# Output projection in seven half-sized products, gain and bias of the first norm on transposed rows, x added by accumulating loads

## The chip, the cores and the metric

One of the cores of a Trainium2 chip runs the whole kernel. The metric is device time in microseconds (us) of one launch. The engines are TensorE (PE, matrix products, with PEld for its weight loads), VectorE (DVE), ScalarE (ACT), GpSimd (POOL, which also issues the DMAs of the software queue) and SyncE (SP, which issues the others). Each executes its own list of instructions in order; semaphores tie the lists together. Matrix products write PSUM banks of 128x512, everything else lives in SBUF tiles of 128 partitions, and weights stream in from DRAM.

## What is computed

One layer of a decoder trunk: 512 tokens, width 1024. Three attention branches are gated and merged (not shown), then:

```python
def layer_norm(x, g, b):
    mu = xf.mean(-1, keepdims=True)
    var = jnp.square(xf - mu).mean(-1, keepdims=True)
    return ((xf - mu) * lax.rsqrt(var + LN_EPS) * g + b).astype(x.dtype)
...
m = mixer(x, ...)          # ends with merged @ w_out
x = layer_norm(DEEPNORM_ALPHA * x + m, ln1_g[i], ln1_b[i])
hid = jax.nn.relu(x @ w_up[i])
c = jnp.square(hid) @ w_down[i]
ple = jax.nn.sigmoid(x @ w_ple_gate[i]) * (p[i] @ w_ple[i])
x = layer_norm(DEEPNORM_ALPHA * x + c + ple, ln2_g[i], ln2_b[i])
```

Everything is float32. The change touches `merged @ w_out`, the first norm, and `p @ w_ple`.

## The kernel before, in words

**Products.** A float32 product is made of three products in a reduced format: each operand is split into a high part h (a cast, ACT: `wh` for weights, line 243) and a remainder l (a subtraction, DVE: `wl`, line 245), and h·h + h·l + l·h is summed in PSUM. Large products are done by Strassen's scheme in seven half-sized products, p = 1 to 7 in the order 1, 2, 7, 6, 4, 5, 3 (`seven`), each for two row tiles r; a half-sized product of one row tile is 12 PE products of 128x512. The summed weight blocks that p5, p6, p7 and p3 need are made in DRAM by the software queue (`sum_steps`), paced by a credit that each item of the program adds to, or by adding a second block onto a loaded one in SBUF (`chained`, line 180).

**The output projection** (`wout_items`, line 897) does not use that scheme: for both column halves and four row tiles tt it runs 24 PE products (lines 909 to 911) from `merged_T`, the split and transposed merge (`turn_item`). The eviction (line 917, DVE) computes y = ALPHA·x + product with its row sum; x comes in eight loads `xn` of 128x512 (256 KB each) by POOL. After the second half of a row tile `ln1_gen(tt)` starts.

**The first norm** (`layer_norm_act`, line 861): row mean (DVE, L866), sum of squares of each half (ACT, L868, into `junk`), variance (DVE, L870 and L871), the power -1/2 (POOL, L872), then for each half (x - mean)·g (DVE, L874) and ·r + b (DVE, L882). After a count of steps by tt, PE transposes the row tile (eight 128x128, line 946); ACT and DVE split it into `x1hT`, `x1lT` (L952, L953), and ACT copies it to `x1r` (L959), of which the operands of the gate's later products are summed (`x_forms`: L1163 and following; t7, t6 and t4 are those of p7, p6 and p4).

**Around it.** The eight items `ple` (p @ w_ple, lines 977 to 979, evicted by ACT at L983) stand behind the output projection and fill PE while the last rows are normed. Then the gate x @ w_ple_gate runs as seven half-sized products in the order 2, 1, 7, 6, 4, 5, 3 (lines 1040 to 1042): its p2 and p1 need the transposed rows alone, p7 needs t7. `gate_rest` multiplies gate and `ple` and adds ALPHA·x1 later.

**Order.** Program order of each engine follows from the recording: an item's eviction is recorded after the next item's products have begun, casts of coming weights are pumped between items, and generators in `pending` take one step at a time. A wait thus holds back all that was recorded behind it on the same engine. POOL issues its DMAs in that order as well, and each of them also waits for the landing of the one eight places ahead of it.

## Time and profile before

| what | value |
|---|---|
| median of 3 runs | 1036.45 us (1035.87 to 1036.88) |
| the profiled execution | 1036.02 us |
| its span, first to last instruction | 1033.9 us |
| mean granted TensorE clock | 0.998 |
| instructions on PE, DVE, ACT, POOL | 5434, 1412, 1012, 271 |
| first product of the output projection | 606.63 us into the span |
| first product of the gate's p7 | 681.46 us into the span |

A time that follows "start" in the timeline counts from the span's first instruction. A group line gives source line, engine, operation, out<-in with shapes, count, then busy time in us and mean duration in ns. The duration of a PE product is longer than the distance to the next one, since products overlap; what a product costs is that distance. The same holds for short operations on ACT and DVE.

### The profile page before, as it was taken

The numbers are of one execution on the slowest core, as the hardware profiler recorded it, in microseconds if no ns is written. First come the engines' busy times: TensorE is split into PE (matmuls) and PEld (weight loads), VectorE is DVE, ScalarE is ACT, GpSimd is POOL, SyncE is SP. The second block draws the span as 40 slices with busy tenths as digits, with TensorE's granted clock in tenths as the row PEclk, the third lists the DMA queues.
The fourth block names the chain that finished last, engine by engine and source line by source line (L and its number), as shares of the span: only waits on it lengthen the run. The fifth ranks groups of instructions, "written<-read, shape, count | busy, mean of one in ns | idle before, by whom it ended". The sixth has DMA issues, their size and how long they took to land.

```text
span 1033.9 us, 15019 instructions
## 1 busy us (share of the span) xinstructions
PE 1025.6 (99%) x5434; PEld 880.3 (85%) x5434; DVE 786.4 (76%) x1412; ACT 592.9 (57%) x1012; POOL 180.5 (17%) x271
## 2 busy tenths in 40 slices
PE   9999999999999999999999999999999999999997
PEld 6888888889888888888888888889999899899886
DVE  7888667769764657779688895798768777777966
ACT  7565544536434646576575743776666556566651
POOL 0002411121211232411011040111111111111001
PEclk9999999999999999999999999999999999999999
DMA  8349969485976999977789895479999999998612
GB/s 310 122 158 272 286 185 220 113 289 151 279 191 214 268 283 292 254 193 199 229 270 222 269 324 197 141 214 336 336 293 312 296 324 339 306 310 273 227 61 81
DMA packets 71321, 249.19 MB, mean 241 GB/s; under 512 B 8808, under 2 KB 9592, under 8 KB 71248
## 3 DMA queue, kind: packets, MB, share of 16 engines
q0 software_dynamic: 32464, 116.21, 45.0%
q1 hardware_dynamic: 38208, 131.13, 35.1%
q8 instruction: 42, 0.69, 0.3%
q10 hardware_dynamic: 576, 0.92, 0.2%
q14 instruction: 31, 0.25, 0.1%
HBM read 246.10 MB, written 98.59 MB: 333 GB/s over the span
## 4 chain that ended last, share of the span: by engine, by line
PE 97%; DVE 2%; ACT 0%; issue 0%; DVEq 0%
PE mm L87 10%; PE mm L89 10%; PE mm L88 10%; PE at L1300 4%; PE at L1301 4%; PE at L1302 4%; PE at L618 3%; PE at L620 3%; PE at L619 3%; PE mm L495 2%; PE mm L497 2%; PE mm L496 2%; PE at L89 1%; PE at L88 1%; PE at L87 1%; PE at L911 1%
## 5 line engine op out<-in xcount | busy, mean ns | idle before, releaser
L243 ACT CAST wh<-raw 128x1024 fp32r<-128x1024 f32 x257 | 268.4, 1049 | 236.3 <-PE mm L88 126.1
L245 DVE TENSOR_TENSOR wl<-raw,wh 128x1024 fp32r<-128x1024 f32 x257 | 312.2, 1222 | 118.3 <-ACT wh L243 117.5
L87 PE MATMUL mm<-xhT,wh 128*128 128x512 f32 x302 | 119.1, 394 | 0.0
L89 PE MATMUL mm<-xhT,wl 128*128 128x512 f32 x302 | 118.3, 392 | 0.0
L88 PE MATMUL mm<-xlT,wh 128*128 128x512 f32 x302 | 118.2, 391 | 0.0
L1300 PE MATMUL at<-wh,hh 128*128 128x512 f32 x188 | 73.7, 392 | 0.0
L1301 PE MATMUL at<-wl,hh 128*128 128x512 f32 x188 | 73.7, 392 | 0.0
L1302 PE MATMUL at<-wh,hl 128*128 128x512 f32 x188 | 73.1, 389 | 0.0
L87 PE MATMUL mm<-x1hT,wh 128*128 128x256 f32 x256 | 72.8, 284 | 0.0
L88 PE MATMUL mm<-x1lT,wh 128*128 128x256 f32 x256 | 72.4, 283 | 0.0
L89 PE MATMUL mm<-x1hT,wl 128*128 128x256 f32 x256 | 72.4, 283 | 0.0
L89 PEld LDWEIGHTS mm<-xhT,wl 128*128 128x128 f32 x302 | 56.7, 188 | 12.0
L87 PEld LDWEIGHTS mm<-xhT,wh 128*128 128x128 f32 x302 | 56.7, 188 | 11.3 <-PE mm L497 0.2
L88 PEld LDWEIGHTS mm<-xlT,wh 128*128 128x128 f32 x302 | 56.8, 188 | 10.8
L87 PEld LDWEIGHTS mm<-x1hT,wh 128*128 128x128 f32 x256 | 48.9, 191 | 1.9
L88 PEld LDWEIGHTS mm<-x1lT,wh 128*128 128x128 f32 x256 | 48.9, 191 | 1.5
L89 PEld LDWEIGHTS mm<-x1hT,wl 128*128 128x128 f32 x256 | 48.9, 191 | 0.0
L1118 POOL DMA_DIRECT2D usum<-in_wu_dram x32 | 28.4, 933 | 106.8 <-DMA usum<-usum 44.4
L1118 POOL DMA_DIRECT2D dsum<-in_wd_dram x28 | 25.4, 928 | 103.0 <-DVE wl L245 63.2
L1302 PEld LDWEIGHTS at<-wh,hl 128*128 128x128 f32 x188 | 35.3, 188 | 7.7
L1300 PEld LDWEIGHTS at<-wh,hh 128*128 128x128 f32 x188 | 35.5, 189 | 6.1
L1301 PEld LDWEIGHTS at<-wl,hh 128*128 128x128 f32 x188 | 35.5, 189 | 5.7
(628 smaller groups left out, 2673.9 us busy)
## 6 DMA issues: line engine op xcount, KB each, us to landing
usum<-in_wu_dram POOLq DMA_DIRECT2D x48, 512.0 KB, 9.1
dsum<-in_wd_dram POOLq DMA_DIRECT2D x42, 512.0 KB, 9.0
raw<-in_wt_dram SPq DMA_DIRECT2D x38, 512.0 KB, 5.4
raw<-usum SPq DMA_DIRECT2D x32, 512.0 KB, 7.8
raw<-dsum SPq DMA_DIRECT2D x28, 512.0 KB, 6.6
raw<-in_wd_dram SPq DMA_DIRECT2D x25, 512.0 KB, 5.8
raw<-in_wu_dram SPq DMA_DIRECT2D x24, 512.0 KB, 7.0
raw<-in_wv_dram SPq DMA_DIRECT2D x18, 512.0 KB, 5.7
```

The source lines that it names most:

```text
L87: nc.tensor.matmul(ps, wh, xh, start=start, stop=False, skip_group_check=True)
L88: nc.tensor.matmul(ps, wh, xl, start=False, stop=False, skip_group_check=True)
L89: nc.tensor.matmul(ps, wl, xh, start=False, stop=stop, skip_group_check=True)
L243: i = nc.scalar.copy(h, raw)
L245: i = nc.vector.tensor_sub(lo, raw, h.bitcast(F32))
L618: nc.tensor.matmul(ps, h[:, q], c["h"][:, n], start=go, stop=False, skip_group_check=True)
L619: nc.tensor.matmul(ps, h[:, q], c["l"][:, n], start=False, stop=False, skip_group_check=True)
L620: nc.tensor.matmul(ps, lo[:, q], c["h"][:, n], start=False, stop=end, skip_group_check=True)
L1118: i = nc.gpsimd.dma_start(o, i, accum_op=OP.add, max_dma_last_dim=4096)
L1300: nc.tensor.matmul(ps, h[:, q], c["h"][:, s], start=go, stop=False, skip_group_check=True)
L1301: nc.tensor.matmul(ps, h[:, q], c["l"][:, s], start=False, stop=False, skip_group_check=True)
L1302: nc.tensor.matmul(ps, lo[:, q], c["h"][:, s], start=False, stop=end, skip_group_check=True)
```

## The change

1. The output projection goes through `seven`. Three of its seven products end in PSUM banks of their own, and a tile of the result is put together in SBUF from two or three evictions. `turn_item` writes plain copies `mr` of the transposed merge; `wout_forms` sums and splits them into the operands m7, m6, m4, m5, m3 (ten casts, ten remainders, six sums).
2. The sums of weight blocks for it are `wsum` in DRAM (eight steps more of 512 KB), and p7 and p3 add a block onto a loaded one.
3. x is carried as x + y/ALPHA, so the norm uses EPS/ALPHA². The tiles of p1 and p7 are evicted by ACT into `wx`, scaled by 1/ALPHA, and x is added to each by an accumulating load of 256 KB; the other four half rows are loaded as `xn` before.
4. The norm normalises without gain and bias by two ACT operations of 128x512 (scale r, bias -mean·r, which POOL multiplies). Gain and bias are put on the transposed rows by eight ACT operations of 128x128 a row tile, with columns from `lncol`; `x1hT` is cast from their result. The row-major x1 gets gain and bias in `gate_rest`, by a multiplication and an addition on DVE for each half row tile.
5. Two of the eight `ple` items move between p2 and p7 of the projection. The loads of ln1_g and ln1_b come later, the steps of the weight sums are paced faster, and the counts of steps before the transposes become 3, 3, 5, 6.

```diff
+        def wout_forms():
+            r11, r12, r21, r22 = [[merged_T[h, th, kp] for kp in range(2)] for h in range(2) for th in range(2)]
...
+            r7 = [slot("mr") for _ in range(2)]
+            for kp in range(2):
+                nc.vector.tensor_sub(r7[kp], r22[kp], r12[kp])
+            form(7, r7)
...
-                hi, lo = slot("mh", F32R), slot("ml", F32R)
-                nc.scalar.copy(hi, ps)
-                nc.vector.tensor_sub(lo, ps, hi.bitcast(F32))
-                merged_T[h, th, kp] = (hi, lo)
+                if not th:
+                    hi, lo = slot("mh", F32R), slot("ml", F32R)
+                    nc.scalar.copy(hi, ps)
+                    nc.vector.tensor_sub(lo, ps, hi.bitcast(F32))
+                    wo_forms.setdefault(1 + h, []).extend(by_k(hi, lo))
+                t = slot("mr")
+                nc.scalar.copy(t, ps)
+                merged_T[h, th, kp] = t
...
-            it.setdefault("rate", 2.8 if j < 25 else 0.0 if j < 31 else 2.6)
+            it.setdefault("rate", 2.8 if j < 25 else 0.0 if j < 31 else 2.6 if j < 49 else 3.2)
...
-            for tt in range(4):
+            for tt in (0, 1) if h else (2, 3):
                 t = slot("xn")
...
+            def operand(cs, p, kp):
+                return chained(cs, p, kp, [a["wo"][kp, i].rearrange("p k n -> p (k n)") for i in range(4)], wsum[kp])
+
+            def row(tt, half, t, ps, sign):
...
+                i = nc.vector.scalar_tensor_tensor(t, ps, sign * INV, t, op0=OP.mult, op1=OP.add,
+                                                   accum_out=x1sum[tt][:, half:half + 1])
...
+            def later(ps, r):
+                for _ in range(3):
+                    yield
+                row(r, 0, s.pop((1, r)), ps, 1.0)
+
+            def done(ps, p, r):
+                if p in (1, 7):
+                    t = s[p, r] = slot("wx")
+                    nc.scalar.activation(t, ps, AF.Copy, scale=INV if p == 1 else -INV)
+                    src = a["xn"][:, r, 0:512] if p == 1 else a["xn"][:, 2 + r, 512:1024]
+                    nc.gpsimd.dma_start(t, src, accum_op=OP.add, max_dma_last_dim=4096)
+                elif p == 2:
+                    pending.append(later(ps, r))
+                elif p == 6:
+                    t = s[6, r] = xn.pop((r, 1))
+                    nc.vector.scalar_tensor_tensor(t, ps, -INV, t, op0=OP.mult, op1=OP.add)
+                elif p == 4:
+                    row(r, 1, s.pop((6, r)), ps, -1.0)
+                elif p == 5:
+                    row(2 + r, 1, s.pop((7, r)), ps, -1.0)
+                else:
+                    row(2 + r, 0, xn.pop((2 + r, 0)), ps, 1.0)
...
+                if (p, r) == (2, 1):
+                    ple_items(range(FIRST))
...
-            layer_norm_act([x1[tt, 0], x1[tt, 1]], x1sum[tt], "ln1_g", "ln1_b", fin)()
-            for _ in range((2, 3, 6, 8)[tt]):
+            nc.vector.tensor_scalar(nmu, sm[:, 0:1], sm[:, 1:2], -1.0 / D, op0=OP.add, op1=OP.mult)
+            for h in range(2):
+                nc.scalar.activation(junk, ts[h], AF.Square, bias=nmu, accum_out=sq[:, h:h + 1])
+            nc.vector.tensor_scalar(r, sq[:, 0:1], sq[:, 1:2], 1.0 / D, op0=OP.add, op1=OP.mult)
+            nc.vector.tensor_scalar(r, r, EPS / ALPHA ** 2, None, op0=OP.add)
+            nc.gpsimd.tensor_tensor(r, r, mhalf, OP.pow)
+            nc.gpsimd.tensor_tensor(c, nmu, r, OP.mult)
+            for h in range(2):
+                nc.scalar.activation(ts[h], ts[h], AF.Identity, scale=r, bias=c)
+            for _ in range((3, 3, 5, 6)[tt]):
                 yield
...
+                    for k in range(2):
+                        n = 4 * h + 2 * kp + k
+                        nc.scalar.activation(r3[:, k, :], tp[:, (2 * kp + k) * P:(2 * kp + k) * P + P], AF.Identity,
+                                             scale=lncol[:, n:n + 1], bias=lncol[:, 8 + n:9 + n])
+                    if tt < 2 or h:
+                        ks = slice(4 * h + 2 * kp, 4 * h + 2 * kp + 2)
+                        o = x1T["b"][:, ks, q]
+                        nc.scalar.copy(o, r3)
+                        nc.vector.tensor_sub(x1Tl["b"][:, ks, q], r3, o.bitcast(F32))
...
                     t = x1[tt, half]
+                    nc.vector.tensor_mul(t, t, lnc["ln1_g"][half])
+                    nc.vector.tensor_add(t, t, lnc["ln1_b"][half])
...
+            todo.extend(two_steps(wsum[m], a["wo"][m]) for m in range(2))
...
-            if 12 <= n < wout_at + 8:
+            if 12 <= n < STEPS_TO:
...
-            if n == wout_at - 1:
+            if n == ple_at:
                 ln_consts("ln1_g", "ln1_b")
```

The order lists show what comes of it. Names are out<-in with a number for each tile; the brackets name the semaphores waited for. First ACT, between row tile 1's and row tile 2's norm. Before, from the copies of row 0 to the squares (L868) of row 2:

```order
L952 CAST x1hT<-at_6329 128x4x128 [waits PE_49]
L952 CAST x1hT<-at_6336 128x4x128 [waits PE_49]
L959 COPY x1r_6343<-at_6329 128x2x128 [waits DVE_49]
L959 COPY x1r_6345<-at_6329 128x2x128
L243 CAST wh_6441<-raw_5975 128x1024 [waits DMAHW2_49,PE_49]
L959 COPY x1r_6347<-at_6336 128x2x128 [waits DVE_49]
L959 COPY x1r_6349<-at_6336 128x2x128
L868 ACTIVATE junk_6352,lsq_6351<-xn_5927,lnm_6353 128x512
L243 CAST wh_6447<-raw_6033 128x1024 [waits DMAHW3_49,PE_49]
L868 ACTIVATE junk_6352,lsq_6351<-xn_5984,lnm_6353 128x512 [waits Activation_49]
```

Now, from row 1's transposed tiles (at_6475, at_6488) to the squares (L999) and the normalising (L1005) of row 2:

```order
L1032 CAST x1hT<-x1r_6437 128x2x128 [waits Activation_49]
L1027 ACTIVATE x1r_6442<-at_6475,lncol 128x128
L1027 ACTIVATE x1r_6452<-at_6488,lncol 128x128 [waits PE_49]
L1032 CAST x1hT<-x1r_6442 128x2x128 [waits Activation_49]
L1027 ACTIVATE x1r_6452<-at_6488,lncol 128x128
L1027 ACTIVATE x1r_6457<-at_6488,lncol 128x128
L1032 CAST x1hT<-x1r_6452 128x2x128 [waits Activation_49]
L1027 ACTIVATE x1r_6457<-at_6488,lncol 128x128
L999 ACTIVATE junk_6505,lsq_6501<-xn_5937,lnm_6502 128x512 [waits DVE_49]
L1032 CAST x1hT<-x1r_6457 128x2x128 [waits Activation_49]
L999 ACTIVATE junk_6505,lsq_6501<-wx_6239,lnm_6502 128x512 [waits Activation_49]
L243 CAST wh_6568<-raw_6362 128x1024 [waits DMAHW7_49,PE_49]
```

Row 2's squares stand behind all of row 1's work on the transposed tiles, and that work is eight small operations and four casts in place of two casts and four copies.

On POOL, around the powers of the four row tiles (`lr` with `mhalf`). Before, the gain and bias loads and then the powers:

```order
L857 DMA ln_b_6020<-in_ln_b_dram 128x512 [waits DMASW1_49]
L1648 DMA pTr_6065<-in_pT_dram 128x512 [waits DMASW2_49,PE_49]
L1648 DMA pTr_6067<-in_pT_dram 128x512 [waits DMASW3_49,PE_49]
L872 TENSOR_TENSOR lr_6253<-lr_6253,mhalf 128x1 [waits DVE_49]
L872 TENSOR_TENSOR lr_6293<-lr_6293,mhalf 128x1 [waits DVE_49]
L1118 DMA dsum_1_145<-in_wd_dram 128x1024 [waits DMASW4_49,DVE_49]
L872 TENSOR_TENSOR lr_6357<-lr_6357,mhalf 128x1 [waits DVE_49]
```

Now (6330, 6377, 6503 and 6538 are row tiles 0 to 3):

```order
L1002 TENSOR_TENSOR lr_6377<-lr_6377,mhalf 128x1 [waits DVE_49]
L1003 TENSOR_TENSOR lc_6378<-lnm_6376,lr_6377 128x1 [waits Pool_49]
L895 DMA ln_g_6528<-in_ln_g_dram 128x512 [waits DMASW1_49,PE_49]
L895 DMA ln_g_6529<-in_ln_g_dram 128x512 [waits DMASW2_49,PE_49]
L895 DMA ln_b_6532<-in_ln_b_dram 128x512 [waits DMASW3_49,PE_49]
L1002 TENSOR_TENSOR lr_6503<-lr_6503,mhalf 128x1 [waits DVE_49]
L895 DMA ln_b_6533<-in_ln_b_dram 128x512
L1003 TENSOR_TENSOR lc_6504<-lnm_6502,lr_6503 128x1 [waits Pool_49]
L1002 TENSOR_TENSOR lr_6538<-lr_6538,mhalf 128x1 [waits DVE_49]
L1003 TENSOR_TENSOR lc_6539<-lnm_6537,lr_6538 128x1 [waits Pool_49]
```

The loads of gain and bias went behind row 1's power, and the last of them, ln_b_6533, behind row 2's; each power is followed by a product.

On DVE, in the queue ahead of the gate's t7. Before, from row 3's normalising (L882) to t7's sums (L1163) and remainder:

```order
L882 SCALAR_TENSOR_TENSOR xn_5929<-xn_5929,lr_6397,ln_b_6019 128x512 [waits Pool_49]
L882 SCALAR_TENSOR_TENSOR xn_5986<-xn_5986,lr_6397,ln_b_6020 128x512 [waits DVE_49]
L245 TENSOR_TENSOR wl_6482<-raw_6205,wh_6481 128x1024 [waits DMAHW6_49,Activation_49]
L953 TENSOR_TENSOR x1lT<-at_6503,x1hT 128x4x128 [waits Activation_49]
L245 TENSOR_TENSOR wl_6545<-raw_6211,wh_6544 128x1024 [waits DMAHW7_49,Activation_49]
L953 TENSOR_TENSOR x1lT<-at_6557,x1hT 128x4x128 [waits Activation_49]
L1163 TENSOR_TENSOR x1r_6514<-x1r_6514,x1r_6510 128x512 [waits Activation_49]
L1163 TENSOR_TENSOR x1r_6516<-x1r_6516,x1r_6512 128x512 [waits Activation_49]
L1167 TENSOR_TENSOR x1r_6510<-x1r_6343,x1r_6510 128x512 [waits DVE_49]
L272 TENSOR_TENSOR t7l_6587<-x1r_6514,t7h_6586 128x512 [waits Activation_49]
```

Now, where ln_b_6533 is first waited for (through DMASW4):

```order
L1001 TENSOR_SCALAR lr_6538<-lr_6538 128x1 [waits DVE_49]
L1088 TENSOR_TENSOR wx_6239<-wx_6239,ln_b_6533 128x512 [waits DMASW4_49]
L245 TENSOR_TENSOR wl_6588<-raw_6366,wh_6587 128x1024 [waits DMAHW1_49,Activation_49]
L1087 TENSOR_TENSOR xn_5937<-xn_5937,ln_g_6528 128x512
L1087 TENSOR_TENSOR xn_5939<-xn_5939,ln_g_6528 128x512 [waits PE_49,Activation_49]
L1087 TENSOR_TENSOR wx_6274<-wx_6274,ln_g_6529 128x512 [waits PE_49,Activation_49]
L1088 TENSOR_TENSOR xn_5937<-xn_5937,ln_b_6532 128x512 [waits DVE_49]
L1088 TENSOR_TENSOR wx_6274<-wx_6274,ln_b_6533 128x512 [waits DVE_49]
L1088 TENSOR_TENSOR xn_5939<-xn_5939,ln_b_6532 128x512
L1087 TENSOR_TENSOR xn_5987<-xn_5987,ln_g_6529 128x512
L1033 TENSOR_TENSOR x1lT<-x1r_6620,x1hT 128x2x128 [waits Activation_49]
L1088 TENSOR_TENSOR xn_5987<-xn_5987,ln_b_6533 128x512 [waits DVE_49]
```

Gain and bias of the row-major tiles (L1087, L1088) stand between the rsqrt of row 3 (L1001) and the remainders of rows 2 and 3; t7's first sum comes six rows on, its remainder five behind that.

More of the change, by code (lines that the diff above doesn't have):

```diff
@@ L601, in mixer_forms, with seven @@
             yield
-        def seven(forms, operand, bank_of, done):
+        def seven(forms, operand, bank_of, done, behind=None, rate=0.35):
             cs = {}
@@ L1485, in trunk @@
         ple_at = len(items)
-        ple_items()
+        ple_items(range(FIRST, 8))
         pleg_items()
@@ L2020, in trunk @@
         DA_TABS = 44
+        STEPS_TO = ple_at - 2
         sum_steps_ = sum_steps()
```

140 lines of the change are left out of this document (78 added, 62 removed).

## Prediction

> **What bounds the kernel now.** I read the page first: the busy shares, then the chain of work that ended last.
>
> ```profile
> PE 1025.6 (99%) x5434; PEld 880.3 (85%) x5434; DVE 786.4 (76%) x1412; ACT 592.9 (57%) x1012; POOL 180.5 (17%) x271
> PE 97%; DVE 2%; ACT 0%; issue 0%; DVEq 0%
> ```
>
> TensorE sets the end. The next view cuts the span into stages (columns: stretch, length, busy time of PE, PEld, DVE, ACT, POOL, granted clock, DMA share, GB/s).
>
> ```profile
> 606.00:658.00 52.00, 52.00 (x246) 43.04 (x245) 36.54 (x64) 20.10 (x35) 8.65 (x16) 1.00 0.60 195
> 658.00:690.00 32.00, 31.99 (x153) 26.56 (x152) 28.24 (x45) 27.27 (x53) 5.75 (x8) 1.00 0.70 208
> 690.00:720.00 30.00, 30.00 (x178) 26.66 (x177) 26.75 (x35) 18.04 (x27) 4.62 (x7) 1.00 1.00 334
> ```
>
> PE never pauses where the change lies, so a product removed is worth its full spacing, and a wait added costs its full length: no later slack takes it back. The second row warns: just after the output projection ACT is busy 85% and DVE 88%, though their shares of the span are 57% and 76%. The timeline of PE gives spacings and the frame (start, duration, engine):
>
> ```profile
> 606.63 0.39 PE L909 MATMUL at<-wh,mh 128*128 128x512 f32 x1
> ...
> 637.63 0.39 PE L910 MATMUL at<-wl,mh 128*128 128x512 f32 x1
> ...
> 646.47 0.39 PE L910 MATMUL at<-wl,mh 128*128 128x512 f32 x1
> ...
> 650.33 1.04 PE L946 MATMUL at<-ident,xn 128*128 128x128 f32 x8
> ...
> 664.39 1.04 PE L946 MATMUL at<-ident,xn 128*128 128x128 f32 x8
> ...
> 681.46 0.39 PE L1040 MATMUL at<-wh,t7h 128*128 128x512 f32 x1
> ```
>
> From 637.63 to 646.47 lie 39 products: 0.2267 us each. Eight transposes in 1.04 us, the last of 0.27, are 0.11 apart. Below, t counts from 606.63, the first product of the output projection; the gate's product p7 starts at t = 74.8. That stretch holds 300 products and 56 transposes: 68.0 + 6.2 = 74.2; the other 0.6, over nine returns from transposes to products, is 0.07 each.
>
> **What the change removes.** The projection goes from 192 products to 168.
>
> ```profile
> L909 PE MATMUL at<-wh,mh 128*128 128x512 f32 x64 | 25.3, 395 | 0.0
> ```
>
> (three such lines of 64.) Up to the gate's p7 there are now 276 products, 56 transposes and 15 returns: 62.6 + 6.2 + 1.0 = 69.8. Without a wait the gain is **5.0 us**.
>
> **What it adds, on ACT first.** ACT rows, spacings as start to start:
>
> ```profile
> 353.46 0.36 ACT L1815 ACTIVATE scr<-at,rr 128x128 f32<-128x128 f32 x1
> 353.71 0.20 ACT L1815 ACTIVATION_READ_ACCUMULATOR scr<-at,rr 128x1 f32 x1
> ...
> 641.10 0.73 ACT L868 ACTIVATE junk<-xn,lnm 128x512 f32<-128x512 f32 x1 [4.80 <-DVE lnm L866]
> ...
> 641.95 0.72 ACT L868 ACTIVATE junk<-xn,lnm 128x512 f32<-128x512 f32 x1
> ...
> 657.32 2.00 ACT L243 CAST wh<-raw 128x1024 fp32r<-128x1024 f32 x2
> ...
> 669.74 0.65 ACT L959 COPY x1r<-at 128x256 f32<-128x256 f32 x2 [0.66 <-DVE x1lT L953]
> ...
> 1021.17 0.39 ACT L1391 CAST rest<-xn 128x256 fp32r<-128x256 f32 x1
> ...
> 1023.01 1.34 ACT L879 ACTIVATE xn<-xn,lr 128x512 f32<-128x512 f32 x2 [1.45 <-POOL lr L872]
> ```
>
> A 128x128 operation from PSUM with a column as scale takes ACT 0.25; a square 0.85 with its accumulator read; a weight cast 0.94 (2.00 for two, less one of 1.06); a 128x512 with a column 0.62 (1.34 - 0.72); a 128x256 cast 0.31 (0.39 less the overlap of some 0.09 seen between neighbours). The trace has no 128x128 with two columns. Its floor is half of two 128x256 copies' spacing, 0.16; its ceiling adds a second column at what one costs, 0.09 here (0.72 against some 0.63 for a plain 128x512): 0.34. I take 0.25, the nearest form. Before, one row's way from the transposes on was two casts and four copies; now it is eight such operations and two or four 128x256 casts, and the normalising itself, two 128x512, has come to ACT from DVE.
>
> I walk rows 0 to 3 along the order lists. Rows 0 and 1: their norm follows p4's evictions (PE ends those at t = 36.6 and 39.8). ACT does row 0's squares around one weight cast, then the small DVE and POOL steps:
>
> ```profile
> 657.90 0.21 DVE L870 TENSOR_SCALAR lr<-lsq 128x1 f32<-128x1 f32 x1
> ...
> 658.68 0.15 DVE L871 TENSOR_SCALAR lr<-lr 128x1 f32<-128x1 f32 x1
> ...
> 674.61 1.29 DVE L1163 TENSOR_TENSOR x1r<-x1r,x1r 128x512 f32<-128x512 f32 x2 [0.44 <-ACT x1r L959]
> ...
> 677.02 1.22 DVE L245 TENSOR_TENSOR wl<-raw,wh 128x1024 fp32r<-128x1024 f32 x1
> 678.16 0.69 DVE L272 TENSOR_TENSOR t7l<-x1r,t7h 128x512 fp32r<-128x512 f32 x1
> ...
> 1022.15 0.42 DVE L1392 TENSOR_TENSOR rest<-xn,rest 128x256 fp32r<-128x256 f32 x1
> ```
>
> ```profile
> 658.29 0.90 POOL L1118 DMA_DIRECT2D dsum<-in_wd_dram  x1 [8.29 <-DVE lr L870]
> ...
> 665.96 0.56 POOL L872 TENSOR_TENSOR lr<-lr,mhalf 128x1 f32<-128x1 f32 x1 [4.48 <-DVE lr L871]
> ```
>
> So DVE spacings are 0.60 for 128x512, 1.14 for a weight remainder, 0.33 for 128x256; a POOL power 0.56 (the new 128x1 product I take at 0.5). Row 0 is normalised at 43.7 where PE wants it at 43.4; row 1 at 48.9 against 48.8: 0.5 lost together.
>
> **Row 2** pays. From row 1's normalising (ends 49.5) ACT must do 13 of the 128x128 operations and 6 casts before it squares row 2: 3.25 + 1.86, until 54.6. Then two squares round a cast, 56.5; rsqrt steps on DVE and POOL with hand-overs, 1.1, 57.6; one DMA issue that stands between power and product on POOL (0.6 for half the size of the 0.90 above), the product, 58.8; first normalised half 59.4. PE, with 54.3 + 0.5, waits 4.7. Its transposes end at 60.7 (nominal 55.2), 12 products follow to 63.5. **Row 3**'s squares stand behind row 2's normalising (60.1): squares and a copy to 62.1, a gain operation and both steps of its rsqrt on DVE to 63.1, POOL 64.2, normalised 64.9: PE waits 1.5 more. Transposes end 66.0, 48 products: the gate's p7 could start at **77.0**.
>
> The Trainium skill ("ScalarE: Activation LUTs", What ACT_TABLE_LOAD costs) gives an ACTIVATE 186 ns + 0.833 ns an element, some 93 ns for each column operand, and some 93 ns of overlap between neighbours: 0.39 us for the new operation. With one column it says 0.29, where the trace has 0.25; by it row 2 would be 1.8 us later and the sum 1.8 us larger.
>
> **DVE and POOL behind it.** The row-major gain and bias, 16 plain 128x512 operations, are moved behind the transposes, into the queue ahead of the gate's forms. One of the first, the bias on row 2's second half (wx), waits for the second ln1_b load, which POOL issues only behind row 2's power, at 57.7. Loads by software queue (KB, median us to landing):
>
> ```profile
> dsum<-dsum POOLq DMA_DIRECT2D x4, 512.0 KB, 6.1
> xn<-in_xn_dram POOLq DMA_DIRECT2D x8, 256.0 KB, 9.3
> ...
> raw<-in_wgm_dram POOLq DMA_DIRECT2D x2, 512.0 KB, 7.1
> ...
> ln_b<-in_ln_b_dram POOLq DMA_DIRECT2D x2, 256.0 KB, 12.4
> ```
>
> At 9.3 it lands at 67.0. Counting the waiting operation, behind that wait on DVE stand, up to the sum that t7 is made of, 11 gain and bias operations (6.6), two weight remainders (2.3), three 128x256 (1.0) and the sum (0.6): 10.5; then four more and t7's remainder, 2.7. PE wants that remainder 4 products (0.9) into p7, so p7 starts no earlier than landing + 12.3 = **79.3**. That is 2.3 beyond the 77.0. The same queue makes t6 late by 0.4. If the load landed at 6.1, the term would be nothing; at 12.4, 5.4.
>
> In a sentence apart: the Trainium skill ("DMA: Bandwidth & Descriptors", Anatomy of one DMA) fits such a load at 2.0 us + bytes / 436e3, 2.6 us for 256 KB, against 9.3 measured; by it this term would vanish and the sum be 2.7 us smaller.
>
> **The accumulating loads.** p1's first tile is evicted at 6.1; the load onto it takes between 6.1 and 12.4 and gates, on DVE, p2's eviction and behind it 5.5 us of queue (pT remainder, a weight, p7's operands) that PE needs at 20.5. So it must land by 15.0; 7.1 (the nearest, a load added into SBUF) gives 13.3, 9.3 gives 15.4, 12.4 gives 18.5. I take 0.3 lost (0 to 3.5). The four loads that put x on p7's tiles land by 44 to 46, when p5's eviction wants them; only above 45 do they delay row 1. The added sums into DRAM (eight of 512 KB) and the ten casts of the new operands and the two chunks more that are loaded lie under PE in a stretch with a DMA share of 0.60, where ACT is busy 20 of 52 us, and two of the eight products with W_p now stand between p2 and p7 as cover; I cost them at nothing, and uncovered a cast would cost 0.5.
>
> **Sum.** 79.3 + 0.4 + 0.3 = 80.0, against 74.8: +5.2. The rest of the kernel is bound by PE as before. The profiled execution took 1036.02 (span 1033.9, 2.1 around it), 0.4 under the median of 1036.45: **1041.2** there, 1041.5 for a median. My bounds: operations at 0.16 and loads at 6.1 put p7 at 75.9, so 1037.5; at 0.34 and 12.4, with 3.5 for the first load, 87.5, so 1048.7, which I cut to 1046.5, as all three would have to be at their ends.
>
> **Rivals.**
> 1. *The rows keep up, faster.* If ACT reaches row 2's squares by 50 instead of 54.6, row 2 is ready when PE comes, and the load and the DVE queue are as much earlier; p7 starts at 69.8 and the time is 1031.4. For it: before, row 2 was normalised at 661.90 and transposed at 664.39, 2.5 us of slack, and ACT idles over 40% of the span. Against it: 19 operations in 0.5 us would be needed; the deciding point is a 128x128 spacing of some 0.05, or another order of arrival than I walked. 0.20.
> 2. *Gain eaten, no change.* Rows 2 and 3 wait, but the ln1_b load lands under 8 us, so DVE decides nothing: p7 at 77.0 or, with 0.16, 75.9: 1037.1 to 1038.6. 0.17.
> 3. *The accumulating loads decide.* They take over 12.4; p7 of the projection waits 4, row 1 another 3, and all later rows move: 1048. The table above shows such landings, but only behind ten queued loads. 0.05.
>
> Forecast itself 0.58. A measurement of this kernel tells 0.2% (2.1 us) from no change. Faster 0.20, same 0.17, slower 0.63. The forecast's own range is 1038.5 to 1046.5; to hold 8 in 10 it must take in the first rival too, so it begins at 1031.5.
>
> **What would show it.** In the changed profile: a PE wait ahead of row 2's transposes of 3.5 to 6, released by ACT's normalising; one of 1 to 2 ahead of row 3's; one of 0 to 5 at the gate's p7, released by DVE, with DVE idle on the ln1_b load just before. The 128x128 operation's spacing at 0.25 and the load's landing at 9.3 are the two sizes. I am wrong if PE stays busy through the norm, or waits mostly at p7 of the projection.

## The result and the profile after: 1066.91 us, slower by 2.9%

| | before | after |
|---|---|---|
| median (range) | 1036.66 us (1035.87 to 1038.48) | 1066.91 us (1066.42 to 1067.72) |
| ratio, 95% interval | | 1.029 (1.0272 to 1.0308) |
| span of the profiled execution | 1033.9 | 1066.0 |
| first product of the output projection | 606.63 | 624.55 |
| first product of the gate's p7 | 681.46 | 710.08 |

Forecast were 1041.5 us and a range of 1031.5 to 1046.5. Slower was right, the size was not: 30 us were lost and not 5. The span falls into three pieces. Up to the projection 17.9 us were lost, in a stretch that the prediction did not treat. From there to the gate's p7 the kernel takes 85.5 us, before 74.8, forecast 79.6. Behind p7 it loses 3.5, forecast 0.4.

First the page of the changed kernel, its busy shares and the chain that ended last:

```profile
PE 1027.8 (96%) x5410; PEld 878.6 (82%) x5410; DVE 802.6 (75%) x1440; ACT 621.3 (58%) x1066; POOL 195.7 (18%) x287
PE 85%; ACT 4%; issue 3%; DMA 3%; DVE 2%; POOL 1%; DVEq 0%; POOLq 0%; ACTq 0%
```

There are 24 products fewer, as the diff says. But PE held 97% of the chain before and now 85%: other engines, DMA and issue end waits that were not there. Which ones, the view of PE's waits tells (line waited at, releaser, us in total, times, longest):

```profile
PE at L1894 <- ACT scr L1898: 15.9, 1, 15.9
PE at L1020 <- ACT xn L1005: 7.2, 2, 6.0
PE at L1020 <- ACT wx L1005: 2.4, 2, 1.3
PE mm L1057 <- DVE pTl L1737: 1.7, 1, 1.7
PE at L1121 <- DVE sg L1130: 1.4, 1, 1.4
...
PE at L1123 <- DVE t6l L272: 0.6, 1, 0.6
PE at L618 <- ACT m7h L271: 0.3, 1, 0.3
```

The largest is a single wait, in an attention branch (L1894) that the change does not edit. The four at L1020 are the transposes of the four rows; the two lines of 1.7 and 0.3 are what the projection waits for ahead of p7. The stages, in the columns of the prediction's windows:

```profile
450.00:590.00 140.00, 131.62 (x595) 109.47 (x596) 110.50 (x176) 86.85 (x141) 21.30 (x28) 0.95 0.84 232
...
606.00:658.00 52.00, 49.98 (x233) 40.02 (x232) 45.04 (x63) 34.02 (x51) 15.22 (x22) 1.00 1.03 288
658.00:690.00 32.00, 23.99 (x112) 18.84 (x110) 20.99 (x45) 25.51 (x54) 9.48 (x13) 0.98 0.68 207
690.00:720.00 30.00, 27.70 (x114) 21.49 (x115) 25.89 (x42) 27.84 (x56) 5.33 (x6) 0.91 0.54 165
```

In the second row the DMA share is 1.03, where it was 0.60. These windows are fixed in time, and the projection begins 18 us later now, so the rows do not show the same work. Ten microseconds at a time, the projection of the kernel before (it begins at 606.63) looks like this:

```profile
606.00:616.00 10.00, 10.00 (x52) 8.12 (x50) 10.00 (x17) 3.18 (x4) 4.93 (x10) 1.00 1.03 343
616.00:626.00 10.00, 10.00 (x53) 8.39 (x51) 6.14 (x11) 2.25 (x4) 2.60 (x5) 1.00 1.06 317
626.00:636.00 10.00, 10.00 (x46) 8.28 (x45) 5.17 (x8) 4.96 (x6) 0.00 (x0) 1.00 0.52 172
636.00:646.00 10.00, 10.00 (x45) 8.27 (x45) 6.23 (x13) 1.93 (x5) 0.57 (x1) 1.00 0.39 149
646.00:656.00 10.00, 10.00 (x49) 8.34 (x48) 7.18 (x16) 5.77 (x14) 0.56 (x1) 1.00 0.01 3
```

Its first 20 us were full before the change, and only what follows had room. In the changed kernel (it begins at 624.55) the share is 1.05, 1.07 and 1.06 in the windows from 626 to 656, and it stays high behind them:

```profile
656.00:666.00 10.00, 10.00 (x45) 8.13 (x45) 8.39 (x13) 6.41 (x11) 3.21 (x4) 1.00 0.98 327
666.00:676.00 10.00, 8.74 (x43) 6.96 (x42) 6.68 (x13) 8.01 (x16) 2.44 (x2) 1.00 0.94 281
```

In the table of stages the clock column shows 0.95 and 0.91 where PE had paused before.

**The wait of 15.9 us, followed back.** Rows of the timeline around it (start, duration, engine, operation; the bracket holds the idle time before it and what ended it):

```profile
437.95 4.49 POOL L376 DMA_DIRECT2D xr<-in_xT_dram  x5
...
455.68 0.69 DVE L581 TENSOR_TENSOR xr<-xr,xr 128x512 f32<-128x512 f32 x1 [17.60 <-DMA xr<-in_xT_dram]
456.29 0.24 DVE L1864 TENSOR_SCALAR mx<-mx 128x2 f32<-128x2 f32 x1
...
456.62 0.40 ACT L1866 ACTIVATE lg<-lg,mx 128x128 f32<-128x128 f32 x1 [19.77 <-DVE mx L1864]
...
458.38 2.08 PE L1894 MATMUL at<-da_v,wT 128*128 128x128 f32 x8 [15.90 <-ACT scr L1898]
```

The loads `xr` carry the input of the next products (L376). Their sums (L581) stand on DVE in front of a small softmax step (L1864) that has nothing to do with them; DVE waits 17.6 us for the loads, ACT for the softmax step, PE for ACT. The loads are late because POOL issues them late. In the kernel before the same loads were issued 22 us earlier:

```profile
415.81 3.34 POOL L376 DMA_DIRECT2D xr<-in_xT_dram  x4
```

Counted along POOL's order, 93 DMAs of weight sums stand ahead of `xr` before and 102 after: the faster pace (`3.2` from item 49 on) puts nine more there. Each DMA of this queue also waits for the landing of the one eight places ahead, as the sixth `xr` load shows; the sum that it waits for was issued at 436.20, eight places earlier:

```profile
445.45 0.71 POOL L376 DMA_DIRECT2D xr<-in_xT_dram  x1 [3.00 <-DMA dsum<-in_wd_dram]
```

### The profile page after: what moved, and what is told of

Its sections match the earlier page's. It is cut to its first block, busy times and chain, and to the rows that moved or that the text cites. A ratio compares the mean times of both kernels' runs of the same rounds, so it can differ in the third digit from the quotient of the medians.

```text
span 1066.0 us, 15094 instructions
## 1 busy us (share of the span) xinstructions
PE 1027.8 (96%) x5410; PEld 878.6 (82%) x5410; DVE 802.6 (75%) x1440; ACT 621.3 (58%) x1066; POOL 195.7 (18%) x287
## 4 chain that ended last, share of the span: by engine, by line
PE 85%; ACT 4%; issue 3%; DMA 3%; DVE 2%; POOL 1%; DVEq 0%; POOLq 0%; ACTq 0%
PE mm L87 10%; PE mm L89 10%; PE mm L88 10%; PE at L1382 4%; PE at L1383 4%; PE at L1384 4%; PE at L618 3%; PE at L620 3%; PE at L619 3%; PE mm L495 2%; PE mm L497 2%; PE mm L496 2%; DMA wx<-in_xn_dram 2%; PE at L89 1%; PE at L88 1%
## 5 line engine op out<-in xcount | busy, mean ns | idle before, releaser
L243 ACT CAST wh<-raw 128x1024 fp32r<-128x1024 f32 x263 | 275.6, 1051 | 225.6 <-PE mm L88 125.9
L245 DVE TENSOR_TENSOR wl<-raw,wh 128x1024 fp32r<-128x1024 f32 x263 | 319.4, 1221 | 111.2 <-ACT wh L243 109.9
L87 PEld LDWEIGHTS mm<-x1hT,wh 128*128 128x128 f32 x256 | 48.9, 191 | 1.9
L89 PEld LDWEIGHTS mm<-x1hT,wl 128*128 128x128 f32 x256 | 48.9, 191 | 0.0
```

The lines of the kernel that those rows point to most:

```text
L87: nc.tensor.matmul(ps, wh, xh, start=start, stop=False, skip_group_check=True)
L89: nc.tensor.matmul(ps, wl, xh, start=False, stop=stop, skip_group_check=True)
L243: i = nc.scalar.copy(h, raw)
L245: i = nc.vector.tensor_sub(lo, raw, h.bitcast(F32))
```

## The experiments

Fourteen kernels. "Span" is that of the profiled execution; each ratio is to the kernel before, run beside it.

| run | median us (range) | ratio, 95% interval | span |
|---|---|---|---|
| e1_pace_back | 1052.90 (1051.88 to 1053.64) | 1.0142 to 1.0172 | 1050.2 |
| e2_pace_alone | 1053.34 (1052.77 to 1054.2) | 1.0147 to 1.0177 | 1051.3 |
| e3_xr_on_sp | 1065.07 (1055.82 to 1066.85) | 1.0212 to 1.0301 | 1054.1 |
| e4_gain_on_dve | 1053.63 (1053.13 to 1053.9) | 1.0147 to 1.0181 | 1051.7 |
| e5_pace_split | 1053.99 (1050.56 to 1054.17) | 1.0147 to 1.0178 | 1052.4 |
| e6_m7_first | 1053.17 (1052.03 to 1054.22) | 1.0142 to 1.0176 | 1052.5 |
| e7_gain_rows_late | 1050.89 (1049.72 to 1052.64) | 1.0127 to 1.0157 | 1048.0 |
| e8_old_norm | 1049.24 (1047.95 to 1050.55) | 1.0109 to 1.0140 | 1048.3 |
| e9_no_accumulating_loads | 1052.82 (1051.5 to 1053.61) | 1.0142 to 1.0173 | 1051.0 |
| e10_sums_out_of_projection | 1048.40 (1047.98 to 1049.7) | 1.0103 to 1.0133 | 1046.5 |
| e11_new_norm_alone | 1043.34 (1042.97 to 1043.9) | 1.0051 to 1.0084 | 1041.7 |
| e12_scheme_alone | 1040.45 (1039.41 to 1040.6) | 1.0024 to 1.0050 | 1037.7 |
| e13_products_behind | 1045.72 (1045.4 to 1047.06) | 1.0072 to 1.0108 | 1045.4 |
| e14_rows_later | 1040.31 (1039.42 to 1041.53) | 1.0024 to 1.0054 | 1037.7 |

### The pace of the weight sums: e1, e2, e3

e1 is the changed kernel with the pace of before. With the slower pace the last weight sums are made after the products that read them, so these products use unfinished weights; the edit is this one number.

```diff
-            it.setdefault("rate", 2.8 if j < 25 else 0.0 if j < 31 else 2.6 if j < 49 else 3.2)
+            it.setdefault("rate", 2.8 if j < 25 else 0.0 if j < 31 else 2.6)
```

> The changed kernel with one number put back: items from the 49th on add 2.6 to the credit of the weight sums again, not 3.2. By the order lists 93 sum transfers then stand ahead of the x loads of the gate's mixer products (xr) on the software queue, as before the change, where the changed kernel has 102. Theory (queue): the 15.9 us wait at the first transposes of a differential-attention block goes, and with it the slower products behind it, 17.9 us in all, since the output projection begins at 624.55 instead of 606.63: about 1049. Rival (bytes): the eight added sums of 512 KB cost their time wherever they stand; the wait moves or shrinks by a few us: 1060 or more.

e2 is the opposite: the kernel before with nothing but the faster pace.

```diff
-            it.setdefault("rate", 2.8 if j < 25 else 0.0 if j < 31 else 2.6)
+            it.setdefault("rate", 2.8 if j < 25 else 0.0 if j < 31 else 2.6 if j < 49 else 3.2)
```

> The kernel before with only the pace of the sums changed (3.2 from the 49th item on), no sum added: 102 sums ahead of xr. Theory (queue): the xr loads are issued some 20 us later, land late, and the same wait appears: 1050 to 1056. Rival (bytes): no transfer was added, so 1036 to 1038.

e3 is the changed kernel with the `xr` loads issued by SP.

```diff
-                        i = nc.gpsimd.dma_start(t.rearrange("p (k t) -> p k t", k=2),
+                        i = nc.sync.dma_start(t.rearrange("p (k t) -> p k t", k=2),
```

> The changed kernel, pace 3.2 kept, with the eight xr loads issued by SyncE instead of POOL. Theory (queue): they no longer stand behind 102 sums; the 15.9 us wait goes, about 1049. Rival (bytes): the DMA engines are full in that stretch (share 0.84 over 450 to 590, more before), so the loads land late from any queue: 1058 or more.

In e1 the wait is gone, the projection starts at 606.23, and 14 us come back. e2 has it without any of the rest. Its largest wait on PE, in the columns of the view of waits (L1811 is the line that is L1894 in the changed kernel):

```profile
PE at L1811 <- ACT scr L1815: 15.4, 1, 15.4
```

And its `xr` loads in the timeline of POOL, 25 us later than in the kernel before:

```profile
440.99 4.30 POOL L376 DMA_DIRECT2D xr<-in_xT_dram  x5
```

One number of the pacing, in a kernel that is otherwise the old one, costs 16.9 us (1053.34 less 1036.47 beside it). That is shown from both sides. e3 settles less: in its profiled execution (1055.82 us) the wait was 5.0 us, but the median is only 1.8 us under that of the changed kernel. The landing times of that execution speak for the traffic. SP issued the loads from 413.67 on, 2 us earlier than POOL in the kernel before, and they took twice as long to land (e3, then the kernel before, median us in the last column):

```profile
xr<-in_xT_dram SPq DMA_DIRECT2D x8, 256.0 KB, 22.8
...
xr<-in_xT_dram POOLq DMA_DIRECT2D x8, 256.0 KB, 11.5
```

Their first sum began at 444.63, 6.2 us later than before. Loads that stayed on POOL's queue slowed down as well: the two of `in_wgm` between 405 and 450 us took 14.5, before 8.5. So with the faster pace the loads are late even when they are not issued late. How much of the 16.9 us is the order on POOL's queue and how much the traffic stays open: whether the other executions of e3 waited in the same place no trace shows.

### Where the sums can go instead: e5, e10

e5 keeps the pace of before up to `xr` and raises it in the seven-product items of the mixers; the sums are complete in time. It is the base of e6 to e10. e10 moves still more of them ahead of the projection and none into it.

```diff
-        def seven(forms, operand, bank_of, done, behind=None, rate=0.35):
+        def seven(forms, operand, bank_of, done, behind=None, rate=0.8):
...
-            it.setdefault("rate", 2.8 if j < 25 else 0.0 if j < 31 else 2.6 if j < 49 else 3.2)
+            it.setdefault("rate", 2.8 if j < 25 else 0.0 if j < 31 else 2.6)
```

> The changed kernel with the pace of the sums 2.6 up to the xr loads (93 sums ahead of them, as before the change) and faster behind them (0.8 for each unit of the mixer's seven products where it was 0.35), so that all sums are recorded in time (125 ahead of the xn loads). Theory (queue): no wait in the attention part; what is left is the output projection and the norm, 1049 to 1053 as in e1. Rival: the nine sums that now lie behind xr only move the wait to a later load: above 1056.

```diff
-        def seven(forms, operand, bank_of, done, behind=None, rate=0.8):
+        def seven(forms, operand, bank_of, done, behind=None, rate=1.15):
...
-            seven(wo_forms, operand, {"first": (2, 1, 7), "last": (2, 4, 3), "get": get}, done, behind, 1.0)
+            seven(wo_forms, operand, {"first": (2, 1, 7), "last": (2, 4, 3), "get": get}, done, behind, 0.0)
```

> As e5, but no weight sum is issued while the projection runs; six more are issued in the mixer products before it (131 sums ahead of the xn loads, 125 in e5). Theory (DMA share of 1.03 to 1.07 from 606 to 636, where it was 0.52 in the last ten of these before the change): loads land 2 to 4 us sooner, the wait ahead of p7 falls below 2 us: e5 less 2 to 5. Rival (order, not bytes: the load is issued late, behind the eviction): within 1.5 us of e5.

e5 starts the projection at 605.77 and loses elsewhere, ahead of p7, at the two products with W_p that stand there as cover. The loads of p stand behind a sum on POOL, ACT waits 2.17 us for them and PE 1.30. Then the remainder of p stands on DVE behind p2's eviction, DVE waits 6.47 us for the accumulating load, and PE 3.13. e10 takes 5.6 us off e5, 4.2 of it ahead of the gate's p7 in the profiled executions (690.55 and 694.79); DVE waits 3.88 for the accumulating load, and PE's two waits become one of 2.14. The sums have to lie somewhere, and in the projection of e5 they cost 4 to 6 us.

### The new norm: e4, e7, e8, e11

e4 is e1 with the 32 gain and bias operations on DVE (its weight sums as in e1).

```diff
-                        nc.scalar.activation(r3[:, k, :], tp[:, (2 * kp + k) * P:(2 * kp + k) * P + P], AF.Identity,
-                                             scale=lncol[:, n:n + 1], bias=lncol[:, 8 + n:9 + n])
+                        nc.vector.tensor_scalar(r3[:, k, :], tp[:, (2 * kp + k) * P:(2 * kp + k) * P + P],
+                                                lncol[:, n:n + 1], lncol[:, 8 + n:9 + n], op0=OP.mult, op1=OP.add)
```

> As e1, and gain and bias of the transposed rows (32 operations of 128x128) done by DVE instead of ACT. Theory (ACT): row 2's squares come 13 operations of 0.35 earlier, the wait ahead of row 2's transposes falls from 6.0 to below 1.5 and PE's half speed behind it goes (2.2): e1 less 6 to 8, 1041 to 1043. Rival (DVE): DVE, busy 65 to 87 per cent there, takes ACT's place as what is waited for: within 2 us of e1.

e7 is e5 with the row-major gain and bias tied behind a late step of the gate.

```diff
-                    nc.vector.tensor_mul(t, t, lnc["ln1_g"][half])
-                    nc.vector.tensor_add(t, t, lnc["ln1_b"][half])
+                    with tc.issue_after(st["low"]):
+                        nc.vector.tensor_mul(t, t, lnc["ln1_g"][half])
+                        nc.vector.tensor_add(t, t, lnc["ln1_b"][half])
```

> As e5, and the 16 row-major gain and bias operations on DVE are tied behind the weight remainder that was recorded last when the gate's p4 is evicted, so none stands among the norms. Theory (DVE's stream of 128x512 operations slows POOL's 128x1 operations; the power of row 3 took 2.68 us in the changed kernel, 0.56 alone): the powers of rows 2 and 3 take 0.6 to 1.0, row 3's wait shrinks by about 1 us; row 2's wait of 6.0 stays above 4.5, as it hangs on ACT: e5 less 1 to 2. Rival (those operations take DVE time that the gate's operands need): the waits at t6 go too, and e5 less 3 or more.

e8 is e5 with the norm of before (with its EPS divided by ALPHA², its loads of gain and bias early, plain copies of the transposed rows).

```diff
-            nc.gpsimd.tensor_tensor(c, nmu, r, OP.mult)
-            for h in range(2):
-                nc.scalar.activation(ts[h], ts[h], AF.Identity, scale=r, bias=c)
...
+            layer_norm_act([x1[tt, 0], x1[tt, 1]], x1sum[tt], "ln1_g", "ln1_b", fin, eps=EPS / ALPHA ** 2)()
```

> As e5, with the projection in seven products and the accumulating loads, but the norm of before: gain and bias row-major within it, on DVE, and six casts and sixteen copies of the transposed rows on ACT in place of 32 operations with columns, 8 normalisations and 12 casts. Theory (ACT's work of the new norm is what rows 2 and 3 wait for): waits ahead of the rows' transposes together below 2.5 us where e1 has 7.7, no slow products behind them: e5 less 7 to 10, 1040 to 1044. Rival (the rows wait since PE comes to them 5 us earlier and p3 ends late): the waits stay above 5.

e11 is the kernel before with the new norm alone.

```diff
-            layer_norm_act([x1[tt, 0], x1[tt, 1]], x1sum[tt], "ln1_g", "ln1_b", fin)()
...
+            nc.gpsimd.tensor_tensor(c, nmu, r, OP.mult)
+            for h in range(2):
+                nc.scalar.activation(ts[h], ts[h], AF.Identity, scale=r, bias=c)
...
+                    nc.vector.tensor_mul(t, t, lnc["ln1_g"][half])
+                    nc.vector.tensor_add(t, t, lnc["ln1_b"][half])
```

> The kernel before with the new norm alone (normalising on ACT, gain and bias on the transposed rows, row-major gain and bias later), the projection, the x loads and the sums as before the change. Theory (ACT): 13 us more work on ACT and the slow POOL operations make rows 1 to 3 late by 3 to 8 us, with PE at half speed behind the longest wait: 1040 to 1047. Rival (the 2.5 us of slack before and 192 products of cover hide it): 1036 to 1038.

e4 gained nothing. Row 2's squares begin at 670.74 in e1 and in e4 alike, and row 2's wait grew from 6.04 to 11.18. Of the growth 2.9 us lie in a tiny POOL operation on row 2's way, 0.94 in e1, that became long while DVE was streaming; the rest is the step before it and the product behind it, which came late or took longer as well. On POOL in e4:

```profile
674.00 3.88 POOL L1002 TENSOR_TENSOR lr<-lr,mhalf 128x1 f32<-128x1 f32 x1 [0.56 <-DVE lr L1001]
```

e7 took 3.1 us off e5 and row 3's wait with it, though the two ranges overlap. It shows what those DVE operations did to POOL. Row 3's power in e5 and in e7:

```profile
678.75 2.69 POOL L1002 TENSOR_TENSOR lr<-lr,mhalf 128x1 f32<-128x1 f32 x1 [4.53 <-DVE lr L1001]
...
677.67 0.57 POOL L1002 TENSOR_TENSOR lr<-lr,mhalf 128x1 f32<-128x1 f32 x1 [3.96 <-DVE lr L1001]
```

e8 took 4.75 off e5, where 7 to 10 were expected. The rows wait 1.2 us in all there, but PE waits 6.2 us for p's operands and 3.8 for an eviction of the projection. What lies behind the gate's p7 is as long as before again (352.7). e11 is the clean measure: the new norm alone costs 7.1 us (1043.34 less 1036.25). Its window of the rows:

```profile
658.00:690.00 32.00, 27.76 (x124) 22.05 (x123) 24.00 (x38) 30.46 (x63) 4.67 (x7) 0.95 0.49 157
```

Its waits on PE (L987 is a product with W_p, L1054 one of the gate):

```profile
PE at L987 <- ACT ple L993: 2.4, 1, 2.4
...
PE at L1054 <- ACT x1r L963: 0.9, 1, 0.9
PE at L987 <- ACT x1r L963: 0.9, 2, 0.6
```

ACT is busy 30.46 of 32 us, where it was 27.27, and every wait in this stage is released by ACT, the largest not for a row but for a PSUM bank that the eviction of a product with W_p (`ple`), queued behind the norm's work, should have freed. ACT is the bound that the prediction named, though it saw it at the rows alone.

### The seven products: e6, e9, e12, e13, e14

e6 is e5 with p2's evictions tied behind the remainders for p7; e9 is e5 without accumulating loads.

```diff
-                row(r, 0, s.pop((1, r)), ps, 1.0)
+                while "m7" not in st:
+                    yield
+                with tc.issue_after(st["m7"]):
+                    row(r, 0, s.pop((1, r)), ps, 1.0)
```

> As e5, and the two evictions of p2 that wait for the accumulating loads are put on DVE behind the remainders of p7's operands. Theory (head of the line): the wait before p7 of the projection (some 4 us in e1, 2.0 in the changed kernel) falls below 0.5 us: e5 less 3 to 4. Rival (the operands themselves are late, since their sums wait for the last transposes and pT): the wait stays above 2.

```diff
-                    t = s[p, r] = slot("wx")
-                    nc.scalar.activation(t, ps, AF.Copy, scale=INV if p == 1 else -INV)
...
-                    nc.gpsimd.dma_start(t, src, accum_op=OP.add, max_dma_last_dim=4096)
+                    t = s[p, r] = xn.pop((r, 0) if p == 1 else (2 + r, 1))
+                    nc.vector.scalar_tensor_tensor(t, ps, INV if p == 1 else -INV, t, op0=OP.mult, op1=OP.add)
```

> As e5, but x is not added by accumulating loads: all eight half rows of x are loaded ahead, as before the change, and p1's and p7's tiles are evicted by DVE in one operation that adds x (four operations of 128x512 on DVE in place of four on ACT and four loads). Theory (the load behind the eviction, 10 us on a full queue, holds p2's eviction at the head of DVE's list): the waits ahead of p7 of the projection (1.3 and 3.1 us in e5) and PE's half speed behind them (some 2 us) go: 1046 to 1049. Rival (the stretch is short of DMA bandwidth, so the x and pT loads are as late): 1051 or more.

e12 joins e8 (old norm), e9 (no accumulating loads) and e10 (no sums in the projection): the scheme by itself.

> The projection in seven products with its sums paced as in e10, x loaded ahead and added by DVE as in e9, and the norm of before: what the change saves without the parts that were found to wait. Theory: the waits at p7 and at the rows are below 3 us together: 1033 to 1037. Rival (the summed and split operands of the projection, 20 operations on DVE and 18 on ACT, are themselves late): 1040 or more.

e6 starts p7 of the projection 5.2 us earlier (626.88, e5 632.04) and ends no earlier: the waits reappear at p4, p3 and the rows. e9 is 1.2 us under e5, inside the two ranges; PE waits 5.2 us for p's operands (4.4 in e5). Neither was a cause by itself. e12 is, with e14, the fastest of the fourteen, and still 4.2 us over the kernel before (1036.25 beside it). The window of its projection:

```profile
606.00:658.00 52.00, 49.68 (x231) 39.33 (x231) 50.83 (x80) 30.37 (x47) 9.49 (x14) 1.00 0.80 256
```

Its waits on PE (L1045 is a product with W_p, L1010 the transposes, L618 a half-sized product):

```profile
PE mm L1045 <- ACT ple L1051: 3.4, 1, 3.4
PE at L1010 <- DVE xn L920: 1.5, 2, 1.0
...
PE at L618 <- DVE xn L953: 1.2, 1, 1.2
```

In all 6.05 us of waits, and DVE busy 50.83 of 52 us where it was 36.54 (the expectation of e13 below says 48.9). To tell a misplaced cover from a full queue, e13 puts all products with W_p behind the projection and holds rows 2 and 3 longer; e14 does the second alone.

```diff
-            for _ in range((3, 3, 5, 6)[tt]):
+            for _ in range((3, 3, 6, 8)[tt]):
...
-        FIRST = 2
+        FIRST = 0
```

> The kernel of e12 (seven products, norm of before, x on DVE, no sums in the projection) with all eight products with W_p behind the projection, as before the change, and counts of 3, 3, 6, 8 steps before the transposes. In e12 PE waits 6.05 us: 1.21 for p5's evictions ahead of p3, 0.99 and 0.49 for normalised rows, 3.36 for a PSUM bank whose eviction ACT holds behind row 3's squares. DVE is busy 48.9 of the 52 us from 606 to 658 (36.5 before the change). Theory order (the products that cover stand in the wrong places): the waits of rows and bank shrink to under 3 us together and the median is 1034 to 1037.5. Rival queue (DVE is full, so what is moved on PE is waited for elsewhere): the waits stay over 5 us in sum, at p7 of the projection or at rows, and the median is 1039 to 1043.

> The kernel of e12 with counts of 3, 3, 6, 8 steps before the transposes; two products with W_p stay between p2 and p7. Theory order: the bank wait of 3.36 us shrinks, since row 2's transposes come one product later and row 3's behind a product of the gate: 1036 to 1038.5. Rival queue: same as e12 or later, 1040 to 1043, with the wait moved to the gate's p7 or its sums.

e13's waits on PE:

```profile
PE at L1010 <- DVE xn L920: 5.1, 2, 3.1
PE at L618 <- ACT m7h L271: 2.9, 1, 2.9
PE mm L1045 <- ACT ple L1051: 2.3, 1, 2.3
```

10.4 us: without the two products between p2 and p7 PE waits for p7's operands, and the rows are later, not earlier. e14 moves the transposes and leaves 3.37 and the total where they were. Both point to the full queue; moving only the cover does not help. That DVE's load is the cause is argued from its busy time, not shown by taking load away, which was not tried. Nor is it told apart from POOL's powers, three of which take 1.47, 1.58 and 0.99 us in e12.

## Why the prediction was right or wrong

**Where the sum failed.** The prediction's step "the added sums into DRAM ... lie under PE in a stretch with a DMA share of 0.60 ...; I cost them at nothing" is the step that failed, in two ways. First, the added sums do not lie where it put them. The changed kernel issues all eight between 205.0 and 337.5 us, and the faster pace that makes room for them acts from item 49 on, far ahead of the projection, where it made the `xr` loads late: 16.9 us (e2). Second, the 0.60 is the mean of 20 us at 1.03 to 1.06 and 30 us at 0.52 and less, and the first 20 us are where the loads of p's operands and the first accumulating loads went. What sums cost there shows in e5, 4 to 6 us (e10 against e5); in the changed kernel all waits ahead of the projection's p7 come to 2.0. The faster pacing stood in the diff and in the text on the change, but the prediction followed POOL's queue only around the rows. The kernel before shows that the slack was small: from the first `xr` load's issue, 415.81, to their first sum, 438.4, lie 22.6 us, and a load took 11.5 to land, so loads that are issued 22 us later had to be late.

Nor is that the whole of the miss. With the pace put back the kernel still loses 16.4 us (e1 against 1036.47 beside it), where 5 were forecast; longer waits at p7 of the projection and at the rows, with half speed behind them, hold most of the rest.

**What was right.** The nominal gain of 5.0 us: e12, with 6.05 us of waits, has a span of 1037.7, and taking these out would leave 1031.6, within 3 us of the 1028.9 that the span before would leave. That is a sum and not a run: no kernel here has shown the gain. That the norm's work on ACT makes the rows late, row 2 most: measured 6.0 us, said 3.5 to 6, released by ACT's normalising. The rival that ACT keeps up is dead (e11).

**Term by term**, in the changed kernel:

| term | predicted | measured |
|---|---|---|
| sums and pace, ahead of the projection | 0 | 17.9 (15.9 and half speed behind it) |
| p7 of the projection | 0.3 | 2.0 (1.7 and 0.3) |
| rows 0 and 1 | 0.5 | 2.4 |
| row 2 | 4.7 | 6.0, and 2.5 of half speed |
| row 3 | 1.5 | 1.2 |
| second ln1_b load at the gate's p7 | 2.3 | 0 |
| behind p7 | 0.4 | 3.5 |

The measured terms, less the 5.0 of the gain, come to 30.5; the spans differ by 32.1, and the 1.6 left are in no listed wait. The predicted ones come to 4.7 and not to the 5.2 of the sum, since the walk also lost 0.5 between the rows' waits, in transposes that end late.

The sizes, in rows of the changed kernel (ACT, POOL):

```profile
679.03 0.79 ACT L1027 ACTIVATE x1r<-at,lncol 128x128 f32<-128x128 f32 x2
...
685.32 0.77 ACT L999 ACTIVATE junk<-xn,lnm 128x512 f32<-128x512 f32 x1
...
698.92 1.50 ACT L1027 ACTIVATE x1r<-at,lncol 128x128 f32<-128x128 f32 x4
...
668.63 1.48 POOL L1002 TENSOR_TENSOR lr<-lr,mhalf 128x1 f32<-128x1 f32 x1 [5.36 <-DVE lr L1001]
670.18 0.97 POOL L1003 TENSOR_TENSOR lc<-lnm,lr 128x1 f32<-128x1 f32 x1
...
676.66 0.55 POOL L1002 TENSOR_TENSOR lr<-lr,mhalf 128x1 f32<-128x1 f32 x1 [5.51 <-DVE lr L1001]
...
688.60 0.58 POOL L895 DMA_DIRECT2D ln_b<-in_ln_b_dram  x1
...
694.04 2.68 POOL L1002 TENSOR_TENSOR lr<-lr,mhalf 128x1 f32<-128x1 f32 x1 [4.52 <-DVE lr L1001]
```

The 128x128 operation with two columns: from 679.03 to the squares at 685.32 ACT does 13 of them and the six casts between, 6.29 us where the prediction had 5.11. Two take 0.79 and four 1.50, so one is 0.35 after another. The value taken was 0.25, which in its row is the distance to the operation's own accumulator read; the ceiling 0.34 was the right end. The Trainium skill's rule ("ScalarE: Activation LUTs", What ACT_TABLE_LOAD costs), by which the prediction worked out an estimate of 0.39, was nearer than the row of the nearest form, and still too high.

The second ln1_b load: issued at 688.60, it landed 4.8 us later against the 9.3 taken; POOL had issued no other for 9 us, while the 9.3 came from loads with others around them. So DVE did not make p7 late. The 3.5 us lost behind p7 are only in part explained: 1.4 and 0.6 are waits of the gate on DVE (`sg`, `t6l`). e8, without the new norm, does not have them. But e7, which pushes gain and bias later, keeps 1.4 and 0.4 of them and 355.5 us behind p7 (355.9 in the changed kernel, 352.4 before), and e11, with the new norm and the old projection, has 353.3. So it takes the norm and the projection together; which operation costs it stays open.

The accumulating loads: the first one was issued at t = 11.1, where the prediction had p1's eviction at 6.1, since ACT had the last copies of the transposed merge and two weight casts in front of it; the load took 6.3, inside the 6.1 to 12.4, and landed at 17.4. That is too late for the 15.0 named as the limit, but e6 and e9 show that without it another wait took its place.

**Half speed** was not in the sum at all. PE behind row 2's wait:

```profile
690.42 1.11 PE L1020 MATMUL at<-ident,xn 128*128 128x128 f32 x4 [6.01 <-ACT xn L1005]
...
692.90 0.63 PE L1056 MATMUL mm<-wl,pTh 128*128 128x512 f32 x1
693.33 0.63 PE L1057 MATMUL mm<-wh,pTl 128*128 128x512 f32 x1
693.76 0.63 PE L1055 MATMUL mm<-wh,pTh 128*128 128x512 f32 x1
...
695.43 0.40 PE L1056 MATMUL at<-wl,pTh 128*128 128x512 f32 x1
```

The distance is 0.43 us where it was 0.2267, up to 695.43. From 690.42 that is 5.0 us for eight transposes and seven products, which at full speed take 2.5; so a wait of 6.0 costs 8.5. Behind the wait of 15.9 it is 2.0 more. Behind the waits of 1.2 to 1.7 us in this kernel nothing of the kind shows. In the other runs it shows behind 1.98 (e3), 2.14 (e10), 2.32 (e13) and 2.44 us (e11), and once behind 1.37 (e5); in e10 it costs some 1.6 us. The Trainium skill ("TensorE: Matmul & The Clock Gate", What's actually happening) has PE at half clock after an idle window of some 3.4 us until it has been busy for about as long. The traces agree on the half clock, but here shorter waits brought it, and 5.0 us passed in the rows above until it ended. A term of 4.7 us for row 2 should have carried this price.

**The other rivals.** The accumulating loads did not decide (e9). "Gain eaten, no change" had its premise, the ln1_b load under 8 us, and failed on rows 0 to 2.

## What to carry to other kernels

A number that paces background transfers acts on everything recorded behind them on the same queue, also far ahead of the code that needed it: before a faster pace is costed at nothing, find the loads whose place in that queue moves, the first reader of each, and what stands behind that reader on its engine. In these runs a wait on PE of some 2 us or more cost its length and about 1.6 to 2.5 us more of half-speed products. When 5 us of products are saved by work on engines that are already over 70% busy in that stage, price the busy time there first (DVE from 36.5 to 50.8 of 52 us in e12, ACT from 27.3 to 30.5 of 32 in e11), since moving the cover around does not make room.

## What the runs showed of the hardware

A 128x1 power on POOL takes 0.55 us in the changed kernel beside a DVE operation that reads one operand from PSUM (row 1), but 1.48 and 2.68, and in e4 3.88 us, while DVE runs 128x512 and 128x1024 operations with two SBUF operands back to back. e7, which moves such operations away, brings row 3's power from the 2.69 of e5 to 0.57. The Trainium skill ("SBUF — State Buffer", SBUF: two separate sides) says that DVE with two SBUF inputs and GpSimd lock one shared pair of ports against each other; the trace agrees in direction, and shows that it can last longer than one DVE operation (1.2 us at most in these stretches).
